# A trunk of mixer, retention and two FFNs on one core: the instructions recorded, and issued in an order computed from TensorE's needs

## The chip, the core and the metric

The kernel runs on one core of one Trainium2 chip. Its engines take instructions from queues of their own, each in order: TensorE (PE in the rows, with its weight loads as PEld), VectorE (DVE), ScalarE (ACT), GpSimd (POOL) and SyncE (SP). POOL and SP mainly issue transfers here, which 16 DMA engines carry out. SBUF is the working memory, PSUM takes TensorE's results. The metric is the time of one launch in device microseconds, as a median of several runs; the profile is of one more execution.

## The reference

One sequence of 512 tokens, width 1024, float32. Two layers of a mixer and a SwiGLU FFN, RMS norms ahead of each, one at the end:

```python
for i in range(DEPTH):                                  # DEPTH = 2
    hn = rmsnorm(h, mix_norm_g[i])
    if i % N_MIXERS == 0:                               # layer 0: gated mixer
        h = h + sgu_mixer(hn, sgu_w_in[j], sgu_w_s[j], sgu_b_s[j], sgu_ln_g[j], sgu_ln_b[j], sgu_w_out[j])
    else:                                               # layer 1: retention, 4 heads, rotary q and k
        h = h + retention(hn, positions, ret_w_in[j], ret_gn_g[j], ret_w_out[j])
    h = h + swiglu(rmsnorm(h, ffn_norm_g[i]), ffn_w_gu[i], ffn_w_down[i])
return rmsnorm(h, final_norm_g)

def swiglu(h, w_gu, w_down):
    a, b = jnp.split(h @ w_gu, 2, axis=-1)              # 1024 -> 2 x 2816
    return (jax.nn.silu(a) * b) @ w_down                # 2816 -> 1024
```

## The kernel before

**Products.** A float32 product is made of three TensorE matmuls (`three`: high by high, high by low, low by high) of operands split in a rounded copy and a rest. For a weight tile ACT makes the copy (`wh`, L216) and DVE the rest (`wl`, L223). On top of that, most matrix products are done as seven block products instead of eight (`seven`; blocks P1, P7, P6, Q4, P5, P2, P3, in an order per unit). P7, P6, Q4 and P5 take sums of weight blocks. A sum is made either by DVE (`plus`, L377) or by the transfer itself: SP loads one block (L346) and a transfer issued by POOL adds the other to it (L349, `accum_op`). The products add up in accumulators X, Y and Z (in the last unit W0 and W1 too). A unit's tile names carry its name: `gu0_3` is a quarter of the FFN's first product, `dn1_1` the last part of its second, `vg`, `qk`, `ro` belong to the retention, `v`, `u`, `so` to the mixer.

**Inputs of a unit.** X (one tile, 4 chunks of 128 tokens) is normalised chunk by chunk. DVE writes xs, TensorE transposes it by the identity into a PSUM tile xT (L667), ACT copies it to the rounded half XH and, for the sums of the seven products, twice more to xr (L671, L704); DVE makes the rest XL (L672). The norm factor (`nf`) is a chain of small steps on ACT and DVE. The retention's output is gated (sg, from pv on DVE, L1236), transposed (zT, L1245), copied to z by ACT (L1247) and summed on DVE (z_S) for the operands z_P6h and z_P6l.

**Space.** Tiles come from pools whose tiles share slots by tag: 38 general ones (`gen`), 5 of 128x512 (`tmp`), and four PSUM tiles ps0 to ps3 of two banks each. A tile that takes a slot waits until the tile before it there has been read.

**Order.** The program is written as jobs with steps (fetch, add, copy, subtract), interleaved by `pipeline` so many jobs ahead of their use. The framework's scheduler (`schedule_with_timeline_sim=True`) then sets the order of instructions on each engine; `tc.high_priority` and `tc.issue_after` correct it at two or three places. Engines stand in order, so one instruction that waits holds those behind it.

The last unit of the second FFN, `dn1_1`, is made by `into_x` with `apart`: in it P7 is summed by transfers, P6 and Q4 by transfers onto the tile before, and P5 by DVE from its own block and the still kept block of P1.

## Time and profile before

| | |
|---|---|
| median of 3 runs | 1200.02 us (1199.03 to 1201.85) |
| the profiled execution | 1203.41 us, span 1201.7 us, mean granted TensorE clock 0.996 |
| TensorE | 1180.0 us busy, 98% of the span, 7374 instructions |
| DVE, ACT, POOL | 960.9 us (80%), 664.6 us (55%), 171.0 us (14%) |
| DMA by load queue, by accumulating queue | 153.37 MB, 38.6%; 70.81 MB, 35.3% of 16 engines' span |

The page's shares are means over the whole span. How long an engine was held up, and by what, stands in the waits view; in the timelines, `[2.18 <-ACT xr_f L704]` behind a row says that its engine stood idle 2.18 us before it and what ended that. The granted clock tells whether a busy TensorE ran at its full speed.

### The profile page before, as it was taken

What the parts mean: (1) busy time and instruction counts of PE and PEld (TensorE: products, weight loads), DVE (VectorE), ACT (ScalarE), POOL (GpSimd) and SP (SyncE); (2) the same over time, 40 slices, a digit from 0 to 9 for tenths busy, and PEclk for the clock granted to TensorE, in tenths of its full rate; (3) what the DMA queues carried; (4) which work ended last, traced back from release to release, by engine and by line L of the source; (5) the groups of instructions that cost most, each with busy time, mean ns of one, the idle gap of its engine ahead of it and who ended that gap; (6) DMA issues with size and microseconds to landing.
All of it is one profiled execution on the core that took longest, in us unless ns stands there. A gap on an engine that the chain in (4) does not pass through costs nothing.

```text
span 1201.7 us, 18455 instructions
## 1 busy us (share of the span) xinstructions
PE 1180.0 (98%) x7374; PEld 1067.4 (89%) x7374; DVE 960.9 (80%) x1143; ACT 664.6 (55%) x842; POOL 171.0 (14%) x151
## 2 busy tenths in 40 slices
PE   8999999999999999999999999999999999999997
PEld 7888899989999987988989898878899989999986
DVE  5587998899977789787885959879788896676897
ACT  5523775554444547555664656566565545535465
POOL 1000122121010130110201111220121210101210
PEclk9999999999999999999999999999999999999999
DMA  9912878898684898777677868877868887856892
GB/s 314 282 47 59 244 161 182 226 228 208 160 205 108 225 184 265 176 163 184 155 202 178 192 155 203 183 151 247 217 153 211 186 216 210 199 135 192 168 245 97
DMA packets 128167, 225.90 MB, mean 188 GB/s; under 512 B 7464, under 2 KB 30032, under 8 KB 128080
## 3 DMA queue, kind: packets, MB, share of 16 engines
q1 hardware_dynamic: 88848, 153.37, 38.6%
q0 software_dynamic: 38944, 70.81, 35.3%
q8 instruction: 58, 0.95, 0.3%
q10 hardware_dynamic: 288, 0.52, 0.1%
q14 instruction: 29, 0.24, 0.1%
HBM read 221.53 MB, written 2.10 MB: 186 GB/s over the span
## 4 chain that ended last, share of the span: by engine, by line
PE 85%; DMA 5%; issue 4%; DVE 2%; ACT 2%; POOL 1%; SPq 0%; DVEq 0%; POOLq 0%; ACTq 0%
PE X_gu L247 6%; PE X_gu L249 6%; PE X_gu L248 6%; DMA wr_gu_P<-in_ffn_w_gu 3%; PE Y_gu L249 3%; PE Y_gu L248 3%; PE Y_gu L247 3%; PE X_dn L247 3%; PE X_dn L248 3%; PE X_dn L249 3%; PE X_vg L247 2%; PE X_vg L248 2%; PE X_vg L249 2%; PE ps_v L247 1%; PE Y_dn L248 1%
## 5 line engine op out<-in xcount | busy, mean ns | idle before, releaser
L216 ACT ACTIVATE wh_gu_P<-wr_gu_P 128x1024 fp32r<-128x1024 f32 x132 | 135.3, 1053 | 87.6 <-DVE wr_gu_P L377 51.0
L223 DVE TENSOR_TENSOR wl_gu_P<-wr_gu_P,wh_gu_P 128x1024 fp32r<-128x1024 f32 x132 | 158.7, 1219 | 25.4 <-ACT wh_gu_P L216 25.1
L349 POOL DMA_DIRECT2D wr_gu_P<-in_ffn_w_gu x50 | 60.9, 1258 | 414.0 <-DVE wl_gu_P L223 196.2
L216 ACT ACTIVATE wh_dn_P<-wr_dn_P 128x1024 fp32r<-128x1024 f32 x72 | 69.1, 980 | 42.6 <-DMA wr_dn_P<-in_ffn_w_down 17.8
L223 DVE TENSOR_TENSOR wl_dn_P<-wr_dn_P,wh_dn_P 128x1024 fp32r<-128x1024 f32 x72 | 79.4, 1128 | 2.7 <-issue 1.1
L223 DVE TENSOR_TENSOR wl_vg_P<-wr_vg_P,wh_vg_P 128x1024 fp32r<-128x1024 f32 x48 | 57.8, 1217 | 14.5 <-ACT wh_vg_P L216 14.4
L349 POOL DMA_DIRECT2D wr_dn_P<-in_ffn_w_down x36 | 41.9, 1239 | 143.6 <-DVE wl_dn_P L223 46.6
L216 ACT ACTIVATE wh_vg_P<-wr_vg_P 128x1024 fp32r<-128x1024 f32 x48 | 49.2, 1055 | 22.8 <-DMA wr_vg_P<-in_ret_w_in 16.7
L349 POOL DMA_DIRECT2D wr_vg_P<-in_ret_w_in x26 | 31.5, 1248 | 207.5 <-DMA wr_vg_P<-in_ret_w_in 73.8
L247 PE MATMUL X_gu<-XH_f,wh_gu_P 128*128 128x256 f32 x176 | 50.6, 288 | 2.2 <-ACT xr_f L704 2.2
L247 PE MATMUL Z_gu<-XH_f,wh_gu_P 128*128 128x256 f32 x176 | 50.0, 284 | 1.4 <-DVE s L1051 1.4
L247 PE MATMUL X_gu<-xP5h_f,wh_gu_P 128*128 128x256 f32 x176 | 50.0, 284 | 0.9 <-ACT u L1026 0.9
L249 PE MATMUL Y_gu<-XH_f,wl_gu_Q 128*128 128x256 f32 x176 | 49.9, 284 | 0.8 <-DVE wl_gu_Q L223 0.8
L248 PE MATMUL X_gu<-XL_f,wh_gu_P 128*128 128x256 f32 x176 | 50.5, 287 | 0.0
L249 PE MATMUL X_gu<-XH_f,wl_gu_P 128*128 128x256 f32 x176 | 50.5, 287 | 0.0
L247 PE MATMUL X_gu<-xP6h_f,wh_gu_P 128*128 128x256 f32 x176 | 50.0, 284 | 0.2
L247 PE MATMUL Y_gu<-XH_f,wh_gu_Q 128*128 128x256 f32 x176 | 49.9, 284 | 0.0
L249 PE MATMUL Z_gu<-XH_f,wl_gu_P 128*128 128x256 f32 x176 | 49.9, 283 | 0.0
L248 PE MATMUL X_gu<-xP6l_f,wh_gu_P 128*128 128x256 f32 x176 | 49.8, 283 | 0.0
L249 PE MATMUL X_gu<-xP3h_f,wl_gu_P 128*128 128x256 f32 x176 | 49.8, 283 | 0.0
L248 PE MATMUL X_gu<-xP3l_f,wh_gu_P 128*128 128x256 f32 x176 | 49.8, 283 | 0.0
L249 PE MATMUL X_gu<-xP6h_f,wl_gu_P 128*128 128x256 f32 x176 | 49.8, 283 | 0.0
(643 smaller groups left out, 4284.5 us busy)
## 6 DMA issues: line engine op xcount, KB each, us to landing
wr_gu_P<-in_ffn_w_gu SPq DMA_DIRECT2D x110, 512.0 KB, 5.3
wr_gu_P<-in_ffn_w_gu POOLq DMA_DIRECT2D x50, 512.0 KB, 7.8
wr_dn_P<-in_ffn_w_down SPq DMA_DIRECT2D x50, 512.0 KB, 5.5
wr_vg_P<-in_ret_w_in SPq DMA_DIRECT2D x40, 512.0 KB, 5.8
wr_dn_P<-in_ffn_w_down POOLq DMA_DIRECT2D x30, 512.0 KB, 7.3
wr_vg_P<-in_ret_w_in POOLq DMA_DIRECT2D x26, 512.0 KB, 6.9
wr_ro_P<-in_ret_w_out SPq DMA_DIRECT2D x20, 512.0 KB, 4.8
wr_qk_P<-in_ret_w_in SPq DMA_DIRECT2D x15, 512.0 KB, 5.9
```

The source lines that it names most:

```text
L216: nc.scalar.activation(h, s, AF.Copy)
L223: nc.vector.tensor_tensor(l, s, f32(h), ALU.subtract)
L247: nc.tensor.matmul(o, ah, bh, start=start, stop=False, skip_group_check=True)
L248: nc.tensor.matmul(o, ah, bl, start=False, stop=False, skip_group_check=True)
L249: return nc.tensor.matmul(o, al, bh, start=False, stop=stop, skip_group_check=True)
L349: nc.gpsimd.dma_start(raw[p, 0, g, s][:, 0:nk, :], source(b, g, s, nk), accum_op=ALU.add)
```

## The change

Every instruction is recorded first, with the tiles that it reads and writes (`Recorder`, `Virtual`, `View`, `EngineProxy` take the places of the framework's objects). `order_of` then computes an order, and `emit` issues the instructions in it under `tc.manual_schedule()`. TensorE's instructions keep roughly the order in which the program names them. Each other instruction gets a latest time (`late`) from a walk backwards over what TensorE needs when, with one instruction at a time on each engine and one DMA transfer at a time; a walk forwards takes on each engine the ready instruction with the earliest latest time, on TensorE the ready one that is named first. Durations in it are formulas in the code. A transfer is counted as 2.2 us to start and as 1.35 us of DMA time for 512 KB (2.7 if it adds), with a margin of 0.6 us, and at most eight fly at once of a kind.

Slots are granted in that walk too, in the order of need, and become tags of their own with one buffer each, so the framework has no choice left. A PSUM tile counts as a whole (`grain`): a reader of a part waits for all that was written before. SBUF tiles are kept apart in 64 parts.

The last unit's P5 gets its sum by transfers. The number of TensorE matmuls is the same; DVE has four additions fewer, POOL four accumulating transfers more, ACT three table loads more. In the trace of the changed kernel all recorded instructions have the line of the recorder's call, so they are told apart by tile names.

```diff
+RESULT = 35
+TO_PE = 55
+HW_DMAS = 8
+class Virtual:
...
+        self.grain = free if psum else max(1, free // 64)
...
+    def realize(self):
+        if self.real is None:
+            extra = {} if self.tag is None else {"tag": f"{self.tag}_{self.granted}", "bufs": 1}
+            self.real = self.pool.real.tile(self.dims, self.dtype, name=self.name, **extra)
+        return self.real
...
+    if name == "dma_start":
+        kind = "add" if "accum_op" in kwargs else "load" if writes else "store"
+        size = n * 4 * (writes or reads)[0].shape[0]
+        busy = {"SP": 450, "POOL": 1200, "ACT": 100}[engine]
+        took = busy
+        slow = max(60, size * (2 if kind == "add" else 1) * 1350 // 524288)
...
+LAND = 2200
+MARGIN = 600
+TABLE = 1290
+def backward(ops, lazy, total, gap):
...
+            q = max(able, key=lambda o: (lazy[o], o.n))
+            queue[:] = [e for e in queue if e[0] is not q]
+            length = q.slow if q.kind else q.busy
+            free[place] = back + length
+            post(free[place], None)
+            q.late = total - back - length - (LAND + q.busy if q.kind else 0)
...
+def order_of(rec, report=None):
...
+                if e == "PE":
+                    op = min((o for o in queue[e] if can(o)), key=lambda o: o.n, default=None)
+                else:
+                    for o in queue[e]:
+                        if can(o):
...
+                            cost = o.late + (3 * TABLE if o.table and o.table != table else 0)
+                            if op is None or (cost, o.n) < best:
+                                op, best = o, (cost, o.n)
...
+    return sorted(ops, key=lambda o: (o.start, o.n))
+def emit(rec):
+    with rec.tc.manual_schedule():
+        for op in order_of(rec):
+            op.call()
...
+    rec = Recorder(tc)
+    nc, tc = rec, rec
...
-            made = seven(name, w, groups, 0, T, A, evac, mid, look, order=order, dma=("P7",), onto=("P6", "Q4"), apart=apart,
+            made = seven(name, w, groups, 0, T, A, evac, mid, look, order=order, dma=("P7", "P5") if apart else ("P7",), onto=("P6", "Q4"), apart=apart,
...
     pipeline(jobs)
-
+    emit(rec)
```

What the order does is seen at four places. First ACT's queue at the start of the second FFN (unit gu1_0), before:

```order
L671 ACTIVATE XH_f_8143<-xT_f_0_8370 128x8x128
L216 ACTIVATE wh_gu_1_P_0_2_8302<-wr_gu_1_P_0_2_8229 128x1024
L216 ACTIVATE wh_gu_1_P_0_0_8333<-wr_gu_1_P_0_0_8237 128x1024
L1026 ACTIVATE s_1_0_8361<-X_gu_0_8307 128x1024
L216 ACTIVATE wh_gu_1_P_0_2_8364<-wr_gu_1_P_0_2_8305 128x1024
L704 ACTIVATE xr_f_0_0_8381<-xT_f_0_8370 128x4x128
L671 ACTIVATE XH_f_8143<-xT_f_1_8446 128x8x128
L704 ACTIVATE xr_f_0_1_8382<-xT_f_0_8370 128x4x128
```

and after:

```order
L309 ACTIVATE wh_gu_0_P_0_0_8386<-wr_gu_0_P_0_0_8091 128x1024
L309 ACTIVATE XH_f_8184<-xT_f_0_8382 128x8x128
L309 ACTIVATE xr_f_0_0_8408<-xT_f_0_8382 128x4x128
L309 ACTIVATE xr_f_0_1_8417<-xT_f_0_8382 128x4x128
L309 ACTIVATE s_1_0_8423<-X_gu_0_8273 128x1024
L309 ACTIVATE wh_gu_0_P_0_2_8433<-wr_gu_0_P_0_2_8152 128x1024
L309 ACTIVATE wh_gu_0_P_0_0_8462<-wr_gu_0_P_0_0_8303 128x1024
L309 ACTIVATE xr_f_0_0_8408<-xT_f_1_8459 128x4x128
```

XH_f and xr_f are copies of the transpose xT_f, s a copy of an accumulator. The two xr_f copies of xT_f_0 now follow its XH copy directly, and one weight copy and the s copy stand behind them. In TensorE's queue there, xT_f_0 has 31 matmuls of Z_gu between it and xT_f_1 before, and 48 after; X_gu of the second half follows xT_f_1 in both.

Second, TensorE's queue at the last head's transposes, before the retention's output product (ro). Before, zT_0:

```order
L247 MATMUL X_ro<-wh_ro_P_0_2_7679,z_P6h_7477 128x512
L248 MATMUL X_ro<-wl_ro_P_0_2_7680,z_P6h_7477 128x512
L1245 MATMUL zT_0_7729<-ident,sg_0_7406 128x128 x8
L249 MATMUL X_ro<-wh_ro_P_0_2_7679,z_P6l_7478 128x512
L247 MATMUL X_ro<-wh_ro_P_0_2_7679,z_P6h_7477 128x512
```

and after, zT_1 and zT_0:

```order
L309 MATMUL Y_ro<-wl_ro_P_0_2_7545,z_P7h_7527 128x512
L309 MATMUL Y_ro<-wh_ro_P_0_2_7533,z_P7l_7536 128x512
L309 MATMUL zT_1_7710<-ident,sg_1_7488 128x128 x8
L309 MATMUL Y_ro<-wh_ro_P_1_0_7558,z_P7h_7569 128x512
L309 MATMUL Y_ro<-wl_ro_P_1_0_7566,z_P7h_7569 128x512
L309 MATMUL zT_0_7728<-ident,sg_0_7548 128x128 x8
L309 MATMUL Y_ro<-wh_ro_P_1_0_7558,z_P7l_7595 128x512
L309 MATMUL Y_ro<-wh_ro_P_1_0_7558,z_P7h_7569 128x512
```

Before, zT_0 stands inside the product P6 (X_ro), with 10 matmuls left until the first one that reads the z_P6 operands of the last group. After, it stands inside P7 (Y_ro), three places behind zT_1, and 46 matmuls lie in between.

Third, DVE's queue ahead of the second pair of transposes for the retention (xs_r is what is transposed, nf_dn its norm factor, turns, turn and frac belong to the rotary tables). Before:

```order
L655 SCALAR_TENSOR_TENSOR nf_dn_1_0_4855<-nf_dn_1_0_4854,nf_dn_1_0_4852 128x1
L659 TENSOR_SCALAR nf_dn_1_0_4856<-nf_dn_1_0_4855 128x1
L527 TENSOR_TENSOR X<-X,X_dn_1_4260 128x512
L660 TENSOR_TENSOR nf_dn_1_0_4857<-nf_dn_1_0_4856,nf_dn_1_0_4854 128x1
L685 SCALAR_TENSOR_TENSOR xs_r_4864<-X,nf_dn_1_0_4857,g_r 128x1024
L642 TENSOR_TENSOR ss_dn_1_341<-ss_dn_1_342 128x1
L652 TENSOR_SCALAR nf_dn_1_1_4879<-ss_dn_1_341 128x1
L653 RECIPROCAL nf_dn_1_1_4881<-nf_dn_1_1_4880 128x1
L655 SCALAR_TENSOR_TENSOR nf_dn_1_1_4882<-nf_dn_1_1_4881,nf_dn_1_1_4879 128x1
L659 TENSOR_SCALAR nf_dn_1_1_4883<-nf_dn_1_1_4882 128x1
L660 TENSOR_TENSOR nf_dn_1_1_4884<-nf_dn_1_1_4883,nf_dn_1_1_4881 128x1
L685 SCALAR_TENSOR_TENSOR xs_r_4891<-X,nf_dn_1_1_4884,g_r 128x1024
```

and after:

```order
L309 SCALAR_TENSOR_TENSOR turns_4852<-ahl,turns_4831 128x512
L309 TENSOR_SCALAR nf_dn_1_1_4861<-ss_dn_1_4604 128x1
L309 RECIPROCAL nf_dn_1_1_4863<-nf_dn_1_1_4854 128x1
L309 TENSOR_TENSOR nf_dn_1_0_4866<-nf_dn_1_0_4849,nf_dn_1_0_4828 128x1
L309 CAST turn_4868<-turns_4843 128x512
L309 SCALAR_TENSOR_TENSOR nf_dn_1_1_4873<-nf_dn_1_1_4863,nf_dn_1_1_4861 128x1
L309 SCALAR_TENSOR_TENSOR xs_r_4876<-X,nf_dn_1_0_4866,g_r 128x1024
L309 TENSOR_SCALAR nf_dn_1_1_4888<-nf_dn_1_1_4873 128x1
L309 SCALAR_TENSOR_TENSOR turns<-ahl,turns_4852 128x512
L309 TENSOR_TENSOR nf_dn_1_1_4899<-nf_dn_1_1_4888,nf_dn_1_1_4863 128x1
L309 TENSOR_TENSOR frac_4902<-turns_4843,turn_4868 128x512
L309 SCALAR_TENSOR_TENSOR xs_r_4910<-X,nf_dn_1_1_4899,g_r 128x1024
```

The rotary operations, which stood some 150 instructions and more earlier before, now stand between the norm's steps.

Fourth, the end of POOL's queue. Before:

```order
L349 DMA wr_dn_1_P_1_0_10960<-in_ffn_w_down 128x2x512
L349 DMA wr_dn_1_P_1_2_10992<-in_ffn_w_down 128x512
L349 DMA wr_dn_1_P_0_0_10888<-in_ffn_w_down 128x2x512
L349 DMA wr_dn_1_P_0_2_10926<-in_ffn_w_down 128x2x512
L349 DMA wr_dn_1_P_1_0_10960<-in_ffn_w_down 128x2x512
L349 DMA wr_dn_1_P_1_2_10992<-in_ffn_w_down 128x512
```

and after:

```order
L309 DMA wr_dn_1_P_0_2_10801<-in_ffn_w_down 128x2x512
L309 DMA wr_dn_1_P_1_0_10834<-in_ffn_w_down 128x2x512
L309 DMA wr_dn_1_P_1_2_10849<-in_ffn_w_down 128x512
L309 DMA wr_dn_1_P_0_0_11211<-in_ffn_w_down 128x2x512
L309 DMA wr_dn_1_P_0_2_11255<-in_ffn_w_down 128x2x512
L309 DMA wr_dn_1_P_1_0_11285<-in_ffn_w_down 128x2x512
L309 DMA wr_dn_1_P_1_2_11294<-in_ffn_w_down 128x512
```

Behind the last transfers onto P6's tiles, which make Q4, stand the four that make P5.

## The prediction

> **What bounds the kernel now.** I read the page first, then TensorE's waits, then TensorE's busy time by stretches of 30 us, and last the timelines around the longest waits. The page gives the bound:

> ```profile
> span 1201.7 us, 18455 instructions
> PE 1180.0 (98%) x7374; PEld 1067.4 (89%) x7374; DVE 960.9 (80%) x1143; ACT 664.6 (55%) x842; POOL 171.0 (14%) x151
> DMA  9912878898684898777677868877868887856892
> ```

> TensorE is busy for 98% of the span, and the change leaves its number of matmuls as it is. What an order can give back is therefore only the time in which TensorE stands still, or runs at less than the full clock. The waits view of TensorE (line and tile, releaser: total us, times, longest) lists the first kind:

> ```profile
> PE xT_in L667 <- DMA X<-in_x: 2.2, 1, 2.2
> PE X_gu L247 <- ACT xr_f L704: 2.2, 1, 2.2
> PE X_ro L247 <- ACT z_P6h L502: 1.6, 1, 1.6
> PE Z_gu L247 <- DVE s L1051: 1.4, 1, 1.4
> PE wake L176 <- POOL eps L170: 1.2, 1, 1.2
> PE X_vg L247 <- ACT sg L1214: 1.0, 1, 1.0
> PE X_gu L247 <- ACT u L1026: 0.9, 2, 0.6
> PE Y_gu L249 <- DVE wl_gu_Q L223: 0.8, 1, 0.8
> PE X_ro L249 <- DVE z_P6l L506: 0.5, 1, 0.5
> PE Y_vg L249 <- DVE xP7l_r L743: 0.5, 1, 0.5
> PE Y_dn L247 <- ACT wh_dn_Q L216: 0.5, 1, 0.5
> PE X_vg L247 <- ACT xr_r L704: 0.5, 1, 0.5
> PE X_dn L247 <- ACT wh_dn_P L216: 0.5, 1, 0.5
> ```

> Two of these (xT_in, wake) belong to the start, 3.4 us together. The other eleven rows add up to 10.4 us, spread over the program, none above 2.2 us. The second kind shows in the first two of these stretches of the windows view (from:to, length, PE busy, PEld, DVE, ACT, POOL, granted clock, DMA share, GB/s):

> ```profile
> 808.90:812.30 3.40, 3.40 (x10) 2.61 (x9) 3.40 (x4) 2.87 (x4) 0.00 (x0) 0.50 1.10 271
> 877.20:880.60 3.40, 3.40 (x18) 3.40 (x18) 2.93 (x3) 3.39 (x4) 0.06 (x1) 0.50 0.02 5
> 900.00:930.00 30.00, 29.65 (x247) 29.44 (x246) 24.95 (x23) 16.94 (x17) 3.65 (x3) 1.00 0.83 205
> 1145.00:1160.00 15.00, 15.00 (x68) 12.43 (x67) 14.51 (x15) 10.74 (x13) 3.35 (x3) 1.00 1.08 261
> ```

> In the first two TensorE is "busy", but at a granted clock of 0.50: each 3.4 us do the work of 1.7, so the two cost 3.4 us that no wait row shows. The first follows the two X_ro waits (1.6 and 0.5 us), the second the 2.2 us wait of X_gu. No other wait after the start is as long as either, and none is followed by such a stretch. I take them as consequences of the stalls. What is to be had is 10.4 + 3.4 = 13.8 us, plus something at the start. The last two rows give the pace at full clock: 29.65/247 = 0.12 us for a matmul of 256 columns, 15.00/68 = 0.22 for one of 512.

> [...]

> **The longest stall, and what the new order does there.** Timelines of TensorE, then of ACT:

> ```profile
> 873.00 1.03 PE L667 MATMUL xT_f<-ident,xs_f 128*128 128x128 f32 x8
> 876.21 0.38 PE L247 MATMUL X_gu<-XH_f,wh_gu_P 128*128 128x256 f32 x1 [2.18 <-ACT xr_f L704]
> ```
> ```profile
> 870.42 2.00 ACT L216 ACTIVATE wh_gu_P<-wr_gu_P 128x1024 fp32r<-128x1024 f32 x2
> 872.31 1.02 ACT L1026 ACTIVATE s<-X_gu 128x1024 f32<-128x1024 f32 x1
> 873.22 1.05 ACT L216 ACTIVATE wh_gu_P<-wr_gu_P 128x1024 fp32r<-128x1024 f32 x1
> 874.16 0.60 ACT L704 ACTIVATE xr_f<-xT_f 128x512 f32<-128x512 f32 x1
> 875.54 0.62 ACT L704 ACTIVATE xr_f<-xT_f 128x512 f32<-128x512 f32 x1
> ```

> X_gu of the second half needs the PSUM slot of the transpose xT_f_0, which comes free when ACT has made its two xr_f copies. In ACT's queue three weight copies and the s copy stand ahead of them (2.00 + 1.02 + 1.05 = 4.1 us). In the changed order both copies follow the XH copy directly, and xT_f_0 stands 48 matmuls ahead of xT_f_1 instead of 31 (0.12 us each): 2 us earlier. Both moves together exceed the 2.18 us by some 4 us: this wait goes, and with it one half-clock stretch, 2.2 + 1.7 = 3.9 us.

> **The second place, ro.** Timelines of TensorE, ACT and DVE there:

> ```profile
> 802.24 1.04 PE L1245 MATMUL zT<-ident,sg 128*128 128x128 f32 x8
> 803.32 1.57 ACT L1247 ACTIVATE z<-zT,gains_cols 128x256 f32<-128x256 f32 x4 [7.49 <-PE zT L1245]
> 806.09 1.06 ACT L502 ACTIVATE z_P6h<-z_S 128x1024 fp32r<-128x1024 f32 x1 [0.25 <-DVE z_S L480]
> 807.17 1.23 DVE L506 TENSOR_TENSOR z_P6l<-z_S,z_P6h 128x1024 fp32r<-128x1024 f32 x1
> 807.20 0.50 PE L247 MATMUL X_ro<-wh_ro_P,z_P6h 128*128 128x512 f32 x1 [1.60 <-ACT z_P6h L502]
> ```

> From the transpose zT_0 to the end of z_P6l takes 808.40 - 802.24 = 6.2 us, and TensorE had other work only until 807.20 - 1.60 = 805.60, or 3.4 us. In the changed order zT_0 follows zT_1 closely and 46 matmuls stand between it and the ones that use z_P6: 46 x 0.22 = 10.1 us. So 1.6 + 0.5 + 1.7 = 3.8 us go. What is late next is zT_1 itself. Its input sg waits for the norm of the last head, and in the new DVE queue 128x1024 operations (1.2 us each, as z_P6l) stand between the small steps of that norm. I count sg ready about 1.2 us after TensorE reaches zT_1; bounds 0 (those operations done early) and 3.7 (three of them in the way). I take 1.2, since TensorE and DVE are both shifted there by the same products.

> **The seven other waits (6.1 us).** The Z_gu wait (1.4) ends with DVE's s addition, which stands in DVE's queue behind a run of three weight subtracts; the new order has these weights made earlier, and transposes one chunk earlier. The sg wait (1.0) is covered by 12 matmuls of X_ro placed between the two halves of P3 (2.7 us). The u, wl_gu_Q, wh_dn and xP7l/xr_r waits are one late operation each, now ordered by when it is due. I let 0.3 remain at Z_gu, 0.5 at u, 0.5 at dn, each between 0 and its old size.

> **A wait that the change adds: the rotary tables.** They are made by some 30 DVE operations of 128x512, like this group, early in the program where DVE has room:

> ```profile
> L869 DVE TENSOR_TENSOR frac<-turns,turn x5: 679/683/684, 287.1 to 331.5; 128x512 f32<-128x512 f32 x5
> ```

> In the new order they stand near the time they are needed, between the small steps of the norm that gives xs_r_0 and xs_r_1, two and then two more of them. At 0.4 to 0.7 us each this delays the transposes xT_r by up to 2.5 us, of which the part beyond the slack, about 1.0, is TensorE's; bounds 0 and 2.5, and 1.0 is the row's 0.683 one and a half times. Behind xs_r wait the transposes, and behind them in TensorE's queue everything.

> **New small waits elsewhere.** The order is fixed on every engine, and PSUM tiles count as wholes. Where the old trace had thirteen waits of a few tenths to two us over 1200 us, I put 1.3 us for those not looked at; bounds 0 and 10.4, all of it.

> **The last unit's P5 by loads.** DVE's four sums go (first and last of them), four accumulating transfers come on POOL's queue. From the timeline, the DMA queues of the page, and the DMA issues past 1100 us:

> ```profile
> 1162.83 1.22 DVE L377 TENSOR_TENSOR wr_dn_P<-wr_dn_P,wr_dn_P 128x1024 f32<-128x1024 f32 x1
> 1172.32 0.68 DVE L377 TENSOR_TENSOR wr_dn_P<-wr_dn_P,wr_dn_P 128x512 f32<-128x512 f32 x1
> 1173.69 0.39 PE L247 MATMUL X_dn<-wh_dn_P,h_P5h 128*128 128x512 f32 x1
> ```
> ```profile
> q1 hardware_dynamic: 88848, 153.37, 38.6%
> q0 software_dynamic: 38944, 70.81, 35.3%
> wr_dn_P<-in_ffn_w_down POOLq DMA_DIRECT2D x9, 512.0 KB, 7.9
> ```

> DVE is freed of 3 x 1.22 + 0.68 = 4.3 us, which is not on the path: no wait for P5's sums is in the list. The accumulating queue took 35.3% of 1201.7 us for 70.81 MB, 5.99 us of all 16 engines per MB (the load queue 3.02), so four blocks of 1.84 MB add 11.0 us of DMA time, much of it in a stretch whose share is already 1.08 (1145 to 1160, above). P5 starts at 1173.69; its base loads were there before, and after an addition of 7.9 us a copy and a subtract (1.06 and 1.22 us) follow. The additions are the last on POOL's queue, behind Q4's. If they are issued by 1160, which is my assumption, they land by 1168, and P5's first weights are ready at 1170.2. I cost the edit at nothing; its cover is the time from 1160 to 1173.69. If queueing uses it up, TensorE waits: bounds 0 and 11.0 us.

> **Tables, start, tail.** ACT loads its function table three times more, at

> ```profile
> L651 ACT ACT_TABLE_LOAD x6 | 7.7, 1283 | 0.1
> ```

> 1.28 us each, 3.9 us on an engine at 55%: nothing, as long as ACT's idle time covers it. At the start the loads are interleaved differently and TensorE's first product stands earlier, but behind another load: 0, between -1.5 and +1.5. The tail behind the last matmul has the same operations: 0.

> **The sum.** Against the profiled execution, 1203.41 us with a span of 1201.7: 13.8 gained; 1.2 (zT_1) + 0.3 + 0.5 + 0.5 + 1.0 (xT_r) + 1.3 (unseen) = 4.8 given back; net 9.0, so 1194.4. That execution is 3.4 us above the median of the runs, 1200.02, so for the median I say 1191.0.

> **Rivals.**
> 1. All waits go and none comes: 1200.0 - 13.8 = 1186.2. For it: every wait listed has cover in the new order. Against it: the two places above where DVE's queue is late.
> 2. As forecast, but the half clock is not tied to those stalls: its two stretches begin 68.3 us apart, twenty times 3.41, as on a fixed grid, so that which idle share a window holds is partly luck. Then 3.4 stays lost: 1194.4. [...]
> 3. No change: in fixed queues one late operation holds all behind it, and new waits return what the old ones gave, 7 to 11 us beyond the 4.8 counted (the old list had 10.4): 1198 to 1202. For it: DVE at 80% has little room to catch up; against: the stretches I followed through both orders have more cover now.
> 4. Slower: the order counts a 512 KB load as 1.35 us of DMA time, the trace gives 3.02 x 0.524 = 1.58. In a stretch with full DMA a plan of 30 us then lags 30 x (1 - 1.35/1.58) = 4.4 us, less its own margin of 0.6: 3.8. The DMA line of the page has four such stretches (digit 9, the first two slices as one), so 15 us of new waits for weights: 1191 + 15 = 1206, more if half clock follows. It decides from 11.4 us on (9.0 + 2.4). Against it: the plan starts transfers as soon as a slot is free, so lag shows only where slots, not due times, let the load wait.

> **How the numbers follow.** Less than 0.2% (2.4 us) either way is about what a measurement of this kernel cannot tell from no change. Chances: as forecast 0.49, all gone 0.08, half clock kept 0.11, no change 0.14, slower 0.18. Faster is the first three, 0.68. The likeliest case alone spans 1187 to 1196 (the bounds of zT_1, xT_r and of half the unseen waits). The range reaches from 1185, a little under "all gone", to 1203, which takes in "no change" and leaves out most of "slower".

> **What would show it.** Right: no wait of X_gu on xr_f near 870, none of X_ro on z_P6h near 800, granted clock 1.00 in all windows past 15 us, waits after the start of about 5 us, the largest at zT and xT_r on DVE. P5 right: no TensorE wait in the last 30 us. Wrong: waits of X or Y tiles on weight copies whose own engine waited for DMA (rival 4), a 0.50 stretch without a stall of 2 us before it (rival 2), or the same total of waits on other lines (rival 3).

## The result and the profile after

The changed kernel takes 1213.17 us (1211.7 to 1218.58), the kernel before 1199.78 in the same runs: a ratio of 1.0117, interval 1.0084 to 1.0150. It is slower by about 14 us, outside the range given. First the page after:

```profile
span 1211.6 us, 18489 instructions
PE 1182.0 (98%) x7374; PEld 1065.7 (88%) x7374; DVE 958.1 (79%) x1139; ACT 677.5 (56%) x845; POOL 175.1 (14%) x155
```

The span grew by 9.9 us, TensorE's idle time in it from 21.7 to 29.6 (span less busy time), its busy time from 1180.0 to 1182.0. No engine got much fuller (ACT 56% instead of 55%). The time is again in waits of TensorE, of which there are other and more (its waits view, line L309 throughout, since the recorder issues everything):

```profile
PE X_gu L309 <- ACT s L309: 4.6, 2, 3.2
PE wake L309 <- POOL ones L309: 2.3, 1, 2.3
PE xT_r L309 <- DVE nf_dn L309: 2.2, 2, 1.5
PE pv L309 <- ACT osq L309: 2.0, 1, 2.0
PE X_ro L309 <- DVE X L309: 1.9, 1, 1.9
PE xT_f L309 <- DVE xs_f L309: 1.7, 2, 1.1
PE ps_v L309 <- ACT XH_in L309: 1.1, 1, 1.1
PE sc L309 <- DVE s L309: 1.0, 1, 1.0
PE mix_ps L309 <- DMA mix_rows<-in_mix_norm_g: 1.0, 1, 1.0
PE X_dn L309 <- ACT s_dn L309: 0.9, 1, 0.9
PE X_so L309 <- DVE X L309: 0.8, 1, 0.8
PE xT_f L309 <- DVE nf_ro L309: 0.7, 1, 0.7
PE sc L309 <- ACT k0h L309: 0.4, 1, 0.4
PE X_gu L309 <- ACT xr_f L309: 0.4, 1, 0.4
PE xT_in L309 <- DMA X<-in_x: 0.3, 1, 0.3
PE X_gu L309 <- ACT u L309: 0.2, 1, 0.2
```

Four rows are of the start (wake, ps_v, mix_ps, xT_in: 4.7 us, 3.4 before). The other twelve make 16.8 us, where eleven made 10.4. Nearly all old rows are gone: z_P6h, sg, Z_gu, wl_gu_Q, the late weights. One of the new ones is worth following back, the longest. ACT's timeline, then TensorE's and POOL's there:

```profile
285.12 1.06 ACT L309 ACTIVATE wh_gu_P<-wr_gu_P 128x1024 fp32r<-128x1024 f32 x1 [0.20 <-DVE wr_gu_P L309]
291.09 1.06 ACT L309 ACTIVATE wh_gu_Q<-wr_gu_P 128x1024 fp32r<-128x1024 f32 x1 [4.91 <-DMA wr_gu_P<-in_ffn_w_gu]
292.05 1.00 ACT L309 ACTIVATE s<-X_gu 128x1024 f32<-128x1024 f32 x1
293.11 0.39 PE L309 MATMUL X_gu<-xP6h_f,wh_gu_P 128*128 128x256 f32 x1 [3.19 <-ACT s L309]
282.09 1.20 POOL L309 DMA_DIRECT2D wr_gu_P<-in_ffn_w_gu  x1 [3.33 <-DVE wl_gu_P L309]
```

ACT stood idle for 4.91 us, with the copy s next in its queue and its accumulator ready. It waited for a weight of Q4, which the transfer issued at 282.09 was still adding up, some 9 us later. TensorE does not need that weight yet; it needs s, since s frees the accumulator for the next product. So the releaser that the waits view names (s) is not the cause: a late landing is, on an engine that takes its instructions in a fixed order. The second s wait (1.44 us, at 1007) has the same ahead of it, ACT idle for 5.25 us until a weight landed at 1005; ahead of the osq wait (at 573) ACT stood idle for 4.21 us until 567.53, for a weight of qk. X_ro is another case. DVE made five weight subtracts in one row (5.76 us from 863.67), and the addition into X that TensorE needed (at 869.34) stood behind them. DVE's timeline, then TensorE's:

```profile
863.67 5.76 DVE L309 TENSOR_TENSOR wl_gu_P<-wr_gu_P,wh_gu_P 128x1024 fp32r<-128x1024 f32 x5
870.07 0.50 PE L309 MATMUL X_ro<-wh_ro_P,z_P3h 128*128 128x512 f32 x1 [1.92 <-DVE X L309]
```

### The profile page after: what moved, and what is told of

It reads as the page before. It is cut to its first block, busy times and chain, and to the rows that moved or that the text cites. A ratio compares the mean times of both kernels' runs of the same rounds, so it can differ in the third digit from the quotient of the medians.

```text
span 1211.6 us, 18489 instructions
## 1 busy us (share of the span) xinstructions
PE 1182.0 (98%) x7374; PEld 1065.7 (88%) x7374; DVE 958.1 (79%) x1139; ACT 677.5 (56%) x845; POOL 175.1 (14%) x155
## 3 DMA queue, kind: packets, MB, share of 16 engines
q1 hardware_dynamic: 88848, 153.37, 38.3%
## 5 line engine op out<-in xcount | busy, mean ns | idle before, releaser
L309 ACT ACTIVATE wh_gu_P<-wr_gu_P 128x1024 fp32r<-128x1024 f32 x132 | 136.9, 1056 | 134.5 <-DMA wr_gu_P<-in_ffn_w_gu 38.0
L309 DVE TENSOR_TENSOR wl_gu_P<-wr_gu_P,wh_gu_P 128x1024 fp32r<-128x1024 f32 x132 | 159.3, 1220 | 62.2 <-ACT wh_gu_P L309 41.9
L309 POOL DMA_DIRECT2D wr_gu_P<-in_ffn_w_gu x50 | 60.8, 1246 | 389.1 <-DMA wr_gu_P<-in_ffn_w_gu 177.0
L309 ACT ACTIVATE wh_dn_P<-wr_dn_P 128x1024 fp32r<-128x1024 f32 (+1 forms) x72 | 69.9, 984 | 58.6 <-PE X_gu L309 22.5
L309 DVE TENSOR_TENSOR wl_dn_P<-wr_dn_P,wh_dn_P 128x1024 fp32r<-128x1024 f32 (+1 forms) x72 | 80.7, 1129 | 15.0 <-ACT wh_dn_P L309 10.0
L309 POOL DMA_DIRECT2D wr_dn_P<-in_ffn_w_down x40 | 46.3, 1193 | 180.0 <-DMA wr_dn_P<-in_ffn_w_down 77.9
L309 ACT ACTIVATE wh_vg_P<-wr_vg_P 128x1024 fp32r<-128x1024 f32 x48 | 49.8, 1059 | 38.5 <-DMA wr_vg_P<-in_ret_w_in 30.3
L309 DVE TENSOR_TENSOR wl_vg_P<-wr_vg_P,wh_vg_P 128x1024 fp32r<-128x1024 f32 x48 | 57.5, 1218 | 9.3 <-ACT wh_vg_P L309 8.4
L309 POOL DMA_DIRECT2D wr_vg_P<-in_ret_w_in x26 | 31.6, 1281 | 190.2 <-DMA wr_vg_P<-in_ret_w_in 96.1
L309 PE MATMUL X_gu<-xP6h_f,wh_gu_P 128*128 128x256 f32 x176 | 50.8, 288 | 4.6 <-ACT s L309 4.6
L309 PE MATMUL X_gu<-XH_f,wh_gu_P 128*128 128x256 f32 x176 | 50.2, 285 | 0.4 <-ACT xr_f L309 0.4
L309 PE MATMUL X_gu<-xP6h_f,wl_gu_P 128*128 128x256 f32 x176 | 50.5, 287 | 0.0
L309 PE MATMUL X_gu<-xP6l_f,wh_gu_P 128*128 128x256 f32 x176 | 50.5, 287 | 0.0
L309 PE MATMUL X_gu<-xP5h_f,wh_gu_P 128*128 128x256 f32 x176 | 50.1, 285 | 0.3 <-ACT u L309 0.2
L309 PE MATMUL X_gu<-xP3h_f,wh_gu_P 128*128 128x256 f32 x176 | 50.3, 286 | 0.0
L309 PE MATMUL Z_gu<-XH_f,wh_gu_P 128*128 128x256 f32 x176 | 50.0, 284 | 0.0
L309 PE MATMUL X_gu<-XL_f,wh_gu_P 128*128 128x256 f32 x176 | 49.9, 284 | 0.0
L309 PE MATMUL X_gu<-XH_f,wl_gu_P 128*128 128x256 f32 x176 | 49.9, 284 | 0.0
L309 PE MATMUL Y_gu<-xP7l_f,wh_gu_P 128*128 128x256 f32 x176 | 49.8, 283 | 0.0
L309 PE MATMUL Y_gu<-XL_f,wh_gu_Q 128*128 128x256 f32 x176 | 49.8, 283 | 0.0
L309 PE MATMUL Z_gu<-XH_f,wl_gu_P 128*128 128x256 f32 x176 | 49.8, 283 | 0.0
L309 PE MATMUL Y_gu<-XH_f,wl_gu_Q 128*128 128x256 f32 x176 | 49.8, 283 | 0.0
## 6 DMA issues: line engine op xcount, KB each, us to landing
wr_gu_P<-in_ffn_w_gu SPq DMA_DIRECT2D x110, 512.0 KB, 5.1
wr_gu_P<-in_ffn_w_gu POOLq DMA_DIRECT2D x50, 512.0 KB, 7.3
wr_dn_P<-in_ffn_w_down SPq DMA_DIRECT2D x50, 512.0 KB, 5.3
wr_vg_P<-in_ret_w_in SPq DMA_DIRECT2D x40, 512.0 KB, 4.9
wr_dn_P<-in_ffn_w_down POOLq DMA_DIRECT2D x33, 512.0 KB, 7.3
wr_vg_P<-in_ret_w_in POOLq DMA_DIRECT2D x26, 512.0 KB, 7.4
wr_ro_P<-in_ret_w_out SPq DMA_DIRECT2D x20, 512.0 KB, 4.8
wr_qk_P<-in_ret_w_in SPq DMA_DIRECT2D x15, 512.0 KB, 4.1
```

Source lines behind the costliest of these rows:

```text
L309: return fn(*[real_of(a) for a in args], **{k: real_of(a) for k, a in kwargs.items()})
```

## The experiments

The theory after the result: **late landings**. The order puts a weight's copy at the moment at which its transfer lands by the order's own reckoning, and what TensorE needs right behind it. Transfers land later than that and with a spread, and each late one holds the queue. The order reckons at least 4.0 us from issue to landing for a 512 KB load (0.45 + 2.2 + 1.35) and 6.1 for an adding transfer (1.2 + 2.2 + 2.7), more where it lines transfers up behind each other. The page after has these medians for the gu weights, by SP's loads and by POOL's additions:

```profile
wr_gu_P<-in_ffn_w_gu SPq DMA_DIRECT2D x110, 512.0 KB, 5.1
wr_gu_P<-in_ffn_w_gu POOLq DMA_DIRECT2D x50, 512.0 KB, 7.3
```

Both kinds together, they land after 3.5 to 10.7 us, 5.8 in the median. Rivals: chains of small norm steps on DVE (the xT rows); P5's transfers; PSUM tiles as wholes; and the mean rate of transfers, which the prediction's fourth rival had named. Ratios below are to the kernel before in the same runs (1201.8 us; the changed kernel: 1.0117).

**Lighter transfers, the same order.** Each adding transfer of more than one 128-row block moves only half of its block; the other half of the second addend is left out, so this kernel's sums are incomplete.

```diff
     def call():
+        if kind == "add":
+            n = (args[0].shape[1] + 1) // 2
+            short = [real_of(a)[:, 0:n, :] for a in args]
+            return fn(*short, **{k: real_of(a) for k, a in kwargs.items()})
```

> The changed order to the row, but every accumulating transfer of more than one 128-row block moves only half of it (the second addend of half the block is left out). Late landings theory: ACT and DVE stand in their fixed queues at a weight whose transfer has not landed, and what TensorE needs stands behind (s in gu0 and gu1, osq at pv, sc); halved transfers land at least 1 us earlier and take about 12 points less DMA share, so the s waits (4.6 us), osq (2.0), sc (1.0), X_ro (1.9) and their half-clock stretch shrink: 1200 to 1206. Norm chains theory: the stalls are DVE's small steps ahead of the transposes, and transfers matter little: 1210 to 1214.

1198.25 us, 0.9974 (0.9961 to 0.9987). Better than was expected: 15 us gone with no instruction in another place. No wait on s, osq or sc is left, and no half-clock stretch (granted clock 0.998 over the execution, 0.995 in the changed kernel). A transfer of the gu weights lands in 4.6 us (median) instead of 5.8, and in 7.7 at most instead of 10.7. The row of xT_r fell from 2.2 to 1.1, those of xT_f from 2.4 to 1.3: half of the waits at the transposes came from the transfers too, and half did not. X_ro (1.5) and X_so (0.8) stayed as well.

**The same transfers, an order with slack for them.**

```diff
-LAND = 2200
+LAND = 4200
```

> The one constant for a transfer's start-up in the order's reckoning goes from 2.2 to 4.2 us, so that weights that have not surely landed are not put ahead in ACT's and DVE's queues. Late landings theory: the s, osq and sc waits go (8.6 us and one half-clock stretch of 1.7), 1201 to 1206. Norm chains theory: the waits at xT and xs stay and nothing else changes much, 1210 to 1214. Rival: the order, told that weights come late, plans its own stalls: 1213 to 1220.

1198.18 us, 0.9969 (0.9957 to 0.9981): one constant takes back all of the loss and a little more. All of TensorE's waits in it:

```profile
PE wake L309 <- POOL ones L309: 2.3, 1, 2.3
PE X_dn L309 <- ACT s_dn L309: 2.3, 2, 1.4
PE X_ro L309 <- DVE X L309: 1.6, 1, 1.6
PE mix_ps L309 <- DMA mix_rows<-in_mix_norm_g: 1.2, 1, 1.2
PE ps_v L309 <- ACT XH_in L309: 1.1, 1, 1.1
PE X_so L309 <- DVE X L309: 0.8, 1, 0.8
PE X_dn L309 <- DVE X L309: 0.5, 1, 0.5
PE X_gu L309 <- ACT u L309: 0.4, 1, 0.4
PE X_so L309 <- DVE y_P6l L309: 0.2, 1, 0.2
```

5.8 us past the start, instead of 16.8. What it did at the stall shown above is in ACT's timeline of this kernel:

```profile
282.23 1.03 ACT L309 ACTIVATE s<-X_gu 128x1024 f32<-128x1024 f32 x1 [0.56 <-PE X_gu L309]
284.13 1.06 ACT L309 ACTIVATE wh_gu_P<-wr_gu_P 128x1024 fp32r<-128x1024 f32 x1 [0.88 <-DVE wl_gu_Q L309]
285.92 1.06 ACT L309 ACTIVATE wh_gu_Q<-wr_gu_P 128x1024 fp32r<-128x1024 f32 x1 [0.73 <-DMA wr_gu_P<-in_ffn_w_gu]
```

s now stands ahead of the Q4 weight, which still waits for its transfer, with nothing urgent behind it. The xT rows are gone too in this order. That does not make them an effect of the transfers alone: lighter transfers left 2.4 of their 4.6 us, and the order with 3200 (below) has 4.4 us at xT_f.

**P5 by DVE again.**

```diff
-dma=("P7", "P5") if apart else ("P7",)
+dma=("P7",)
```

> The changed kernel with the last unit's P5 summed by DVE again, as before. If the P5 transfers cost time, 1205 to 1210. If not (the trace shows no TensorE wait in the last 190 us), 1212 to 1215, or a few us more if DVE's four sums are missed at the end: to 1218.

1224.1 us, 1.0184 (1.0159 to 1.0209), 0.7% or some 8 us slower than the changed kernel. I had allowed up to 5 us. Its waits view has new rows, all of the last unit's P2, and SP's timeline the four loads of P2's weights:

```profile
PE Z_dn L309 <- ACT wh_dn_P L309: 2.1, 1, 2.1
PE Z_dn L309 <- DVE wl_dn_P L309: 1.7, 2, 0.9
PE Z_dn L309 <- DVE h_P2l L309: 0.8, 1, 0.8
1148.25 7.32 SPq L309 DMA_DIRECT2D wr_dn_P<-in_ffn_w_down  x4
```

The loads go out between 1148.25 and 1155.57, and TensorE stands at P2 from 1155 on: 4.6 us in these rows, and half clock behind them (granted clock 0.89 from 1155 to 1170, so 1.7 us of these 15). In the changed kernel the same four go out between 1142 and 1147. That the raw tiles of P1, kept for P5's sum, hold the slots is my reading of it; no run took the slots alone.

**P5 by transfers in the old order.** The same edit in the other direction, in the kernel before.

> The kernel before, order by the framework's scheduler, with only the last unit's P5 summed by transfers. Theory: undoing P5 cost the changed kernel 11 us since the raw blocks of P1, kept for P5's sum, hold slots that P2's loads wait for in that order; the order before had no wait there, so P5 alone gives -1 to +2 us: 1199 to 1204. Rival: P5 by transfers is worth much in itself: 1190 to 1196.

1203.9 us, 1.0020 (1.0010 to 1.0029): within what was expected, 0.2% slower and no gain. P5's transfers are not the loss, and in the old order they are no gain. The changed order is 8 us worse without them.

**PSUM in parts.**

```diff
-self.grain = free if psum else max(1, free // 64)
+self.grain = max(1, free // 64)
```

> The changed kernel with PSUM tiles reckoned in 64 parts, as SBUF tiles are, instead of as wholes. If wholes made the stalls (readers that wait for a whole accumulator), 1203 to 1208. If not, 1210 to 1216: another order of the same kind, with its own late landings.

1258.47 us, 1.0472 (1.0451 to 1.0494). Neither theory had this. The longest rows of its waits, and TensorE's and ACT's timelines at one small case:

```profile
PE X_gu L309 <- DVE s L309: 12.3, 8, 4.9
PE pv L309 <- ACT osq L309: 7.1, 7, 2.3
55.13 0.69 ACT L309 ACTIVATE v<-ps_v,ry_n 128x512 f32<-128x512 f32 x1 [0.53 <-PE ps_v L309]
55.88 0.50 PE L309 MATMUL ps_v<-wl_v,XH_in 128*128 128x512 f32 x1 [0.78 <-ACT v L309]
```

The order lets TensorE go on with one half of the accumulator ps_v while ACT reads the other half into v. In the trace TensorE stops one matmul into that half until ACT's read ends (55.13 + 0.69 = 55.82), so at this place the issued program still keeps the tile as a whole. That all of the 45 us is of this kind is my reading; the other rows were not followed. Reckoning PSUM as wholes is, in any case, no cost of the change: without it the kernel is 3.5% slower.

**The mean rate, alone and with the slack.**

```diff
-        slow = max(60, size * (2 if kind == "add" else 1) * 1350 // 524288)
+        slow = max(60, size * (2 if kind == "add" else 1) * 1580 // 524288)
```

> The changed kernel with the order's price for a transfer's DMA time at 1580 ns per 512 KB, the mean of the trace, instead of 1350; the start-up stays at 2.2 us. If it is the mean rate that the order has wrong (the prediction's fourth rival by its own price), as good as the longer start-up: 1197 to 1201. If it is the spread of the landings around that mean, for which only slack helps, the s and osq waits stay in part: 1203 to 1212.

1207.78 us, 1.0058 (1.0038 to 1.0077). The rate that the trace gives recovers 0.6 points of the 1.17, not all.

> Both: start-up 4.2 us and 1580 ns per 512 KB. Late landings theory: with the start-up at 4.2 us the landings already have their slack, and the rate adds little: 1196 to 1200. Rival: an order told that transfers are scarcer loads earlier and holds slots longer, and stalls elsewhere: 1201 to 1206.

With `LAND = 4200` as well: 1199.14 us, 0.9980 (0.9969 to 0.9991). Beside 0.9969 for the slack alone, the right rate adds nothing. So it was a later reckoned landing that the order lacked, of which a slower reckoned rate gives some.

**Slack of another kind.**

```diff
-RESULT = 35
-TO_PE = 55
+RESULT = 235
+TO_PE = 255
```

> The changed kernel with 0.2 us more reckoned between any two dependent operations of different engines (35 to 235 ns, to TensorE 55 to 255), the transfers as in the change. If what the order lacks is slack of any kind, its small steps and queues get it here and the stalls go: 1198 to 1204. If it is slack on landings alone, the s, osq and sc waits stay: 1210 to 1220, since a chain of six small steps is now reckoned 1.2 us longer than it is.

1214.83 us, 1.0112 (1.0096 to 1.0128): nothing, with other rows (u 3.0, xr_f 2.5) in place of the old ones. 0.2 us between operations of the engines does not help; the slack has to be on the landings.

**Which landings, and how much.** A term per kind added to `LAND` (`MORE = {"load": 0, "add": 2000, "store": 0}`, and `{"load": 2000, "add": 0, "store": 2000}`), then 3200 and 5200 for both kinds.

> The 2 us more only for accumulating transfers, plain loads as in the change. In the changed kernel's trace the two s waits and the half-clock stretch behind the first (6.3 us) trace back to an accumulating transfer, osq, sc and X_ro (4.9 us and a stretch of 1.7) to loads. If that holds and the other stalls follow from these: 1204 to 1208.

1208.02 us, 1.0055 (1.0037 to 1.0073).

> The 2 us more only for plain loads. By the same reading osq, sc and X_ro go and the s waits stay: 1204 to 1209. Rival: loads are the greater part of the bytes and of the queue, and all comes with them: 1197 to 1201.

1209.54 us, 1.0066 (1.0043 to 1.0089). The two kinds have near equal parts, 0.6 and 0.5 points, as was expected. My list of which waits would stay held only in part. With additions alone the s waits fell from 4.6 to 0.4, but X_ro stayed in both runs (2.0 and 2.1), and with loads alone the longest wait is a Y_dn of 3.4 us, at a place that had none. Every edit makes another order, and a late landing then meets another queue. The sum of the stalls goes with the slack, not the single place.

> Half the dose: start-up 3.2 us. If stalls shrink with the slack given, between the change and 4.2: 1199 to 1205. If the spread of landings has to be covered nearly whole (up to 5 us beyond the reckoning in the change's trace): 1205 to 1210.

1201.38 us, 0.9995 (0.9982 to 1.0009).

> Start-up 5.2 us. If more slack still helps: 1195 to 1198. If 4.2 already covers most landings and the order now plans stalls of its own for want of slots: 1198 to 1204.

1201.23 us, 0.9999 (0.9989 to 1.0009). From 2.2 over 3.2 and 4.2 to 5.2 us the ratios are 1.0117, 0.9995, 0.9969, 0.9999: most comes with the first microsecond, which is about what the medians above lie past the least that the order reckons (1.1 and 1.2 us). How much of the loss belongs to the spread around the median alone, no run separates. At 5.2 the waits view has a stall of 2.0 us (X_gu on XL_f), and the granted clock of the profiled execution is 0.995 where it is 0.998 at 4.2. By these rounded clocks some 3.6 us more (0.003 of 1199.3, an estimate) were lost to half clock, and the spans differ by 2.9 (1199.3 and 1196.4). Whether the larger slack made this or another order's chance, no run shows. The best kernel of all is the changed one with 4.2, 0.3% faster than before.

## Why the prediction was wrong

**What held.** Both places that I followed through the orders came out as worked out. There is no X_gu wait on xr_f at the start of the second FFN and no X_ro wait on z_P6h, and at ro TensorE is full (its busy time in the 30 us where it was 27.87):

```profile
780.00:810.00 30.00, 29.99 (x140) 24.38 (x140) 26.89 (x37) 22.12 (x33) 10.07 (x9) 1.00 0.91 166
```

The zT_1 wait that I put at 1.2 did not come (0). The Z_gu, u and dn rests, put at 1.3 together, are 0, 0.2 and 0.9. P5 costs nothing on TensorE's path: no wait row lies past 1010 us. I did not see, though, that the new order needs it (8 us, above).

**The step that failed: "New small waits elsewhere", 1.3 us.** The rows at places I had not looked at are s 4.6, osq 2.0, X_ro 1.9, xT_f 1.7 and 0.7, sc 1.0 and 0.4, X_so 0.8, xr_f 0.4: 13.5 us. The bound I had set there, 10.4, was too low as well. It came from the waits in the old trace, which are no measure of those in a new order. What stood in the place of this term: s and osq, 6.6 us, are ACT held by landings later than the order reckons, with what TensorE needs behind. X_ro, and half of the rows at the transposes, are DVE's queue, and stay with lighter transfers. With 4200 for 2200 the rows past the start are 5.8 in all, about the 4.8 that I had for the whole program.

**The second: the half clock, 3.4 us.** The gain was taken as certain once its two stalls were gone. Two new stalls (s at 293, X_ro at 870) brought two new stretches, so nothing of it came back. That half clock comes behind such a stall held: 1.7 us each, behind windows with 1.91 and 1.92 us of idle time (last section).

**The third: xT_r, 1.0 us.** It measured 2.2, within the bound of 2.5, but the most of it is not the wait that I had worked out:

```profile
484.72 1.06 PE L309 MATMUL xT_r<-ident,xs_r 128*128 128x128 f32 x8 [1.55 <-DVE nf_dn L309]
503.11 1.07 PE L309 MATMUL xT_r<-ident,xs_r 128*128 128x128 f32 x8 [0.67 <-DVE nf_dn L309]
```

Only the second row is at the transposes with the rotary operations ahead: 0.67 us, where I had 1.0. The first, 1.55 us, is at the pair before, where weight subtracts stand between the norm's steps (the last, wl_qk at 482.17, takes 1.21 us) and no rotary operation does. The mechanism of the term was right, and the size of the row came near by luck.

**The start** was put at 0 and cost 1.3 in its rows. With 12.2 (13.5 less 1.3), 3.4, 1.3 and 1.2, less 1.2 at zT_1 and 0.2 at the other rests, 16.7 of the 18.9 us between 1194.4 and the profiled 1213.34 are named. Nearly all of the rest, 2.0 us, is in TensorE's busy time, 1182.0 us for the same 7374 matmuls that took 1180.0 before, though both traces have 3.4 us lost at half clock. The sum had no term for that, and why they took longer no run shows.

**A count.** The "seven other waits" are eight rows; their sum, 6.1 us, is right.

**The rivals.** The fourth, slower by transfers that land later than the order reckons, was the right one, at 0.18. Its price, 1206, was worked from the mean rate and from full stretches. The runs show that the rate alone brings back half (1207.78) and slack on each landing all. The spread of the single landing was in the trace that I had: transfers of the gu weights took 3.5 to 12.5 us, 6.0 in the median. "Against it" I had written that slots, not due times, would let the lag show. That was the wrong place to look: the lag shows in the queue of the engine that waits. Of the second rival, the grid fits both traces (20 steps of 3.41 us between the two stretches before, 169 after), the luck of the phase fits one stall of 2.2 us that no half clock followed (last section), and 3.4 us did stay lost. But in neither kernel's trace did a stretch come among TensorE's products without a stall before it.

## What to carry to other kernels

A static order in which every instruction is just in time is held up by each duration that comes out longer than reckoned. Where the durations of one resource spread (here transfers, for the gu weights before 3.5 to 12.5 us about a median of 6.0), check the reckoned duration against the trace first, and then try slack between landing and first use: here 1 to 2 us of it took back the loss, and a slower mean rate alone half. When you judge a new order, do not only follow the old waits through it: list for each in-order engine what stands behind an operation that waits for a transfer, and who needs that. The waits view names the last link; look one engine further back before naming the cause.

## What the runs showed of the hardware

```profile
805.49:808.90 3.41, 1.28 (x5) 0.70 (x5) 3.41 (x4) 3.16 (x4) 1.22 (x2) 1.00 0.79 100
873.75:877.16 3.41, 1.23 (x11) 1.00 (x10) 3.41 (x4) 3.39 (x6) 0.00 (x0) 1.00 0.00 0
```

Windows view of the kernel after, then of the one with P5 undone, then of the one with slack for loads alone, each window one step long:

```profile
291.20:294.61 3.41, 1.50 (x12) 1.50 (x13) 1.80 (x2) 3.41 (x4) 0.70 (x1) 1.00 0.97 368
294.62:298.02 3.40, 3.40 (x18) 3.40 (x17) 2.28 (x3) 1.92 (x3) 1.73 (x2) 0.50 0.58 86
868.05:871.46 3.41, 1.49 (x7) 1.17 (x7) 3.33 (x6) 2.05 (x4) 1.20 (x1) 1.00 0.21 26
871.47:874.87 3.40, 3.40 (x12) 2.72 (x11) 1.74 (x3) 0.96 (x2) 0.96 (x1) 0.50 1.04 239
```
```profile
866.00:869.41 3.41, 2.14 (x16) 1.82 (x14) 3.41 (x4) 1.76 (x2) 0.44 (x1) 1.00 0.15 26
869.42:872.82 3.40, 2.48 (x11) 2.04 (x12) 2.50 (x6) 1.97 (x4) 0.75 (x1) 1.00 0.60 71
872.83:876.24 3.41, 3.41 (x29) 3.33 (x28) 3.31 (x8) 0.72 (x2) 1.20 (x1) 1.00 1.08 313
```
```profile
850.15:853.57 3.42, 1.50 (x11) 1.45 (x12) 3.42 (x5) 0.89 (x2) 0.73 (x1) 1.00 1.05 403
853.57:856.98 3.41, 3.41 (x21) 2.89 (x20) 3.02 (x3) 2.12 (x4) 1.70 (x2) 1.00 1.02 310
```

In the kernel after, the idle time of the windows ahead is 1.91 and 1.92 us, all from stalls of 3.2 and 1.9 us, and the half clock follows. With P5 undone a stall of 2.2 us, longer than the second of these, lies across the edge of two windows (1.27 and 0.92 idle), and the clock stays at 1.00. So of these two stalls the one of 1.9 us cost 1.7 us more (half of 3.41) and the one of 2.2 us nothing more, and what differs in the views is where they lie in the windows.

The idle time of the window alone does not tell the cases apart: behind 1.91 us came half clock in the kernel after, behind 1.92 us with slack for loads alone it did not, and neither behind 1.60 us in the kernel after (window 571.10 to 574.51, TensorE busy 1.81 of 3.41; clock 1.00 in the next).
